# Program order on VectorE and ScalarE between the feed-forward network and the expert loop, with the shared weight parts moved behind the routing

## The chip, the cores and the metric

One core of a Trainium2 chip runs the whole kernel. The metric is the device time of one execution in microseconds (us); the kernel before was run three times. The engines are named as in the profile: PE (TensorE, matrix products), DVE (VectorE), ACT (ScalarE), POOL (GpSimd), and SP (SyncE), which here does nothing but issue the DMAs of the weights. Every engine works off its own instructions in one fixed order; what differs between the two kernels is mostly that order.

## The reference

A two-layer trunk over 256 tokens of width 1024. Layer 0 is attention and a dense SwiGLU network. Layer 1 is a pooling mixer and then eight experts, two of them per token:

```python
for i in range(DEPTH):
    m_lat = (jax.nn.silu(c) @ mod_w[i] + mod_b[i])[:, None, :]
    sh1, sc1, g1, sh2, sc2, g2 = jnp.split(m_lat, 6, axis=-1)
    h_lat = modulate(x, sh1, sc1)                      # h * (1 + scale) + shift
    y_lat = attention_mixer(...) if even else pool_mixer(h_lat, pool_w[j], pool_scale[j])
    x = layer_norm(DEEPNORM_ALPHA * x + g1 * y_lat, ln1_g[i], ln1_b[i])
    h = modulate(x, sh2, sc2)
    y = swiglu(h, ...) if even else moe_swiglu(h, moe_router[j], ...)
    x = layer_norm(DEEPNORM_ALPHA * x + g2 * y, ln2_g[i], ln2_b[i])

def moe_swiglu(h, router, wg, wu, wd):
    top_val, top_idx = lax.top_k(h @ router, TOP_K)    # 2 of 8 experts per token
    ...                                                # softmax of the two, one-hot gates
    for e in range(N_EXPERTS):
        out = out + gates[..., e:e + 1] * swiglu(h, wg[e], wu[e], wd[e])
```

The matrix `mod_w` of a layer has 6 x 1024 columns. The kernel works it off in tiles of 512 columns, the "modulation tiles".

## The kernel before, in words

**Layer 0's feed-forward network** is worked off in chunks of hidden columns, weights streamed from HBM. Each weight tile is split into a rounded part and a remainder (`split`, L154 on ACT, L155 on DVE) and each product is made of three matmuls (`mm3`, L159 to L161). Beside it the twelve modulation tiles of layer 1 are computed, one at a time. A tile can be made on PE (`mod_sums`, L297: 16 matmul records, then one addition on DVE, L331) or on DVE (L336: eight multiply-adds over 512 columns). `next_mod` chooses: tiles 0, 1, 3, 5, 7, 9 and 11 go to PE. The last of them, tile 11, gives the gate row `g2b`; its matmuls stand behind the pooling mixer (L297 and then L356).

**Between the network and the experts**, in this order on PE: the sums over the tokens that the mixer's shift needs (`sums`, L911), the bias rows (L1015), the pooling matmuls (L1024, L1025), the mixer's matmuls (`mix`, L1040), tile 11. DVE adds the residual, takes mean and variance for each half of the tokens and normalizes (`norm` with `rstd1`, L189 to L196 and L1002 to L1009), once before the mixer and once behind it.

**The experts' beginning** (`moe`). The normalized tokens are transposed (L168), modulated and split into a rounded part and a remainder. The router's matmuls (L1150, L1160) give the logits `L`. From them DVE makes, in some twenty small instructions, the selection `sel`, the counts, the ranks and the list `idx`, which says which expert is worked off in which rank. SP reads `idx` (L1260) before it can issue any expert weight's DMA. A first piece of all eight experts, the "head" of 64 hidden columns each, does not depend on the routing: its weights are already on the chip. It is computed in four groups j = 0 to 3, each with a gate part and an up part: `front_parts(j)` splits the weights, `front_sums(j)` does the matmuls (48 for a group), `hidden(j)` multiplies by the gates and applies the activation. Then `gather` picks the tokens of the first step (L1292), and `front(steps[0])` is the first work of the **expert loop** (L1585 gate and up, L1645 back), which streams the rest of the weights, 1 MB a tile, through twelve slots: six of a pool of their own, and six in which the head's weights lie at first.

**What sets the order.** Between `order.enter_context(...)` behind the network's start and `pe_order.close()`, PE's instructions stand as the program is written. DVE's and ACT's are put in order by a scheduler that takes what it expects to be ready first, so that weight splits stand between the small instructions of the routing.

Of the kernel before, what the change touches and what calls it, by code (L numbers as in the profile page):

```python
# [17 lines left out]
P = 128  # L18
D = 1024
KB = D // P  # L20
S = 256
# [81 lines left out]
class Trunk:  # L103
# [79 lines left out]

    def rstd1(self, mv):

        V = self.nc.vector
        one = lambda nm, dt=F32: self.sm.tile([P, 1], dt, name=nm)
        ve, vh, i, y, t, nb = one("ve1"), one("vh1"), one("rsi1", I32), one("rsy1"), one("rst1"), one("nb1")
        V.tensor_scalar(ve, mv[:, 1:2], LN_EPS, None, op0=OP.add)  # L189
        V.tensor_scalar(i, ve.bitcast(I32), 1, None, op0=OP.logical_shift_right)  # L190
        V.tensor_scalar(y.bitcast(I32), i, -1.0, float(0x5f3759df), op0=OP.mult, op1=OP.add)
        V.tensor_scalar(vh, ve, -0.5, None, op0=OP.mult)
        for _ in range(3):
            V.scalar_tensor_tensor(t, y, vh, y, op0=OP.mult, op1=OP.mult)
            V.scalar_tensor_tensor(y, t, 1.5, y, op0=OP.add, op1=OP.mult)
        V.scalar_tensor_tensor(nb, mv[:, 0:1], -1.0, y, op0=OP.mult, op1=OP.mult)  # L196
        return y, nb
# [602 lines left out]
    def residual_stats(self, x, y, alpha=ALPHA):  # L800
# [4 lines left out]
        for h in range(2):  # L805
            for tt in range(2):
# [10 lines left out]
    def layer0_ffn_and_rest(self, xn1):  # L817
        tc, nc, I = self.tc, self.nc, self.I
        with ExitStack() as st0:
# [5 lines left out]
            with ExitStack() as st:  # L825
# [79 lines left out]
                def sums():  # L905

                    m2 = [tmp.tile([P, 4, S], F32, name="wh") for _ in range(2)]
                    for half in range(2):
                        t = self.ps()
                        for s in range(2):  # L910
                            nc.tensor.matmul(t, self.ones, self.A[:, s, 2 * half:2 * half + 2].rearrange("p g t -> p (g t)"), start=(s == 0),  # L911
                                             stop=(s == 1))
                        for c in range(4):
                            k = 4 * half + c
                            nc.scalar.activation(m2[half][:, c], t[:, (c // 2) * S:(c // 2 + 1) * S], AF.Copy, scale=self.ab1[:, 1, k:k + 1])
                    return m2
# [63 lines left out]
                order = ExitStack()  # L980
# [11 lines left out]
                m2 = sums()  # L992

                yp = [[self.acc() for h in range(2)] for tt in range(2)]

                def norm(tt, y, alpha):

                    mv, st = self.sm.tile([P, 2], F32, name="mv1"), self.sm.tile([P, 2, 6], F32, name="bst")
                    for h in range(2):
                        z = x[:, tt, hf(h)]  # L1000
                        if alpha == 1.0:
                            nc.vector.tensor_add(z, z, y(h))  # L1002
                        else:
                            nc.vector.scalar_tensor_tensor(z, z, alpha, y(h), op0=OP.mult, op1=OP.add)
                        nc.vector.bn_stats(st[:, h], z)
                    nc.vector.bn_aggr(mv, st)
                    r, nb = self.rstd1(mv)
                    nc.vector.tensor_scalar(x[:, tt, hf(0)], x[:, tt, hf(0)], mv[:, 0:1], r, op0=OP.subtract, op1=OP.mult)
                    nc.scalar.activation(x[:, tt, hf(1)], x[:, tt, hf(1)], AF.Identity, bias=nb, scale=r)  # L1009

                for tt in range(2):
                    norm(tt, lambda h: accs[tt][h], 1.0)
# [36 lines left out]
            self.moe(x, g2b, head, order)  # L1049
# [32 lines left out]
    def moe(self, xn, g2b, head, pe_order):  # L1082
# [19 lines left out]

        outs = []

        def front_parts(j):
            wg, wu, _ = head[j // 2]
            js = slice((j % 2) * P, (j % 2 + 1) * P)
            parts = []
            for w in (wg, wu):
                wH, wL = [tmp.tile([P, KB, P], F32R, name="wh", bufs=6) for _ in range(2)]  # L1110
                self.split(wH, wL, w[:, :, js])
                parts.append((wH, wL))
            return parts

        with tc.high_priority():
            parts0 = front_parts(0)

        def front_sums(j, between=None):
            parts = front_parts(j) if j else parts0
            outs.append(t := self.ps())  # L1120
            for ks in ([range(2 * k2, 2 * k2 + 2) for k2 in range(4)] if between else [range(KB)]):
                if between:
                    between(ks[0] // 2)
                for (wH, wL), c0 in zip(parts, (0, S)):
                    for k in ks:
                        self.mm3(t[:, c0:c0 + S], wH[:, k], wL[:, k], hd[0][k // 4][:, k % 4], hd[1][k // 4][:, k % 4], k == 0, k == KB - 1)

        zs = []

        def turn(k2):  # L1130
            z = tmp.tile([P, 512], F32, name="a")

            def cp(d, t):
                for u in range(2):
                    self.to_h3(d[:, u * S:(u + 1) * S], t[:, u * S:(u + 1) * S], 2 * k2 + u, V if u else None)
            self.transposes(z, [xn[:, tt, (2 * k2 + u) * P:(2 * k2 + u + 1) * P] for u in range(2) for tt in range(2)], cp)
            self.split(*[h[k2 // 2][:, 2 * (k2 % 2):2 * (k2 % 2) + 2] for h in hd], z.rearrange("p (u q) -> p u q", u=2))
            zs.append(z)


        part = self.acc()
        V.memset(part[:, 0:S], 0.0)

        def route(k2):
            if k2 < 2:
                turn(k2 + 2)
            for u in range(2):
                k = 2 * k2 + u
                q = k % 4
                nc.tensor.matmul(part[q * 32:q * 32 + E, 0:S], self.rt[:, k], zs[k2][:, u * S:(u + 1) * S], start=(k < 4), stop=(k >= 4),  # L1150
                                 skip_group_check=True)

        for k2 in range(2):
            turn(k2)
        front_sums(0, route)
# [516 lines left out]
```

## Time and profile before

| | |
|---|---|
| runs of the kernel before | 1464.86, 1470.41, 1473.06 us (median 1470.41) |
| the profiled execution | 1471.24 us, its span 1469.0 us |
| PE busy in the span | 1370.8 us (93%) |
| DVE busy | 713.9 us (49%) |
| ACT busy | 465.1 us (32%) |
| POOL busy | 105.7 us (7%) |
| read from HBM | 461.87 MB, 315 GB/s over the span |

The profile gives, for one execution, when each instruction ran. A "stretch" below is counted in us from the span's start. PE's share is high, but a share over the span is a mean over stages with different limits: the attention (to about 280), the network (to 485), the stretch of the change (485 to 550) and the expert loop (to 1469). A row of the timeline gives start, length, engine, line, operation, result and operands with their shapes, the count, and in brackets the idle time before it with what ended it.

### The profile page before, as it was taken

To read this page: it belongs to the slowest core of one execution; us is meant where nothing else is said; L and a number is where in the kernel's file an instruction comes from. 1 tells how busy PE (TensorE), PEld (TensorE's weight loads), DVE (VectorE), ACT (ScalarE), POOL (GpSimd) and SP (SyncE) were. 2 spreads that over 40 slices of the span, in tenths; PEclk is the share of its full clock that TensorE was granted. 3 is DMA by queue.
4 is the path that set the end of the run, shared out by engine and by line. 5 is a ranking of instruction groups with operands and counts; after the bars stand their busy time and mean duration, and the time that the engine had idled before them with its cause. 6 is when DMAs were issued, how large, how long until landed. Compare 5 with 4: busy or idle time off the path is not lost. (4 is left out here: it accounts for less than half of the span.)

```text
span 1469.0 us, 22110 instructions
## 1 busy us (share of the span) xinstructions
PE 1370.8 (93%) x8833; PEld 846.9 (58%) x8833; DVE 713.9 (49%) x1158; ACT 465.1 (32%) x692; POOL 105.7 (7%) x65
## 2 busy tenths in 40 slices
PE   6899879699999999999999999999989999999995
PEld 4776546589899685655664333343333345667762
DVE  2678794856767773765573101012110015556663
ACT  3443453443343352544451000010000013445541
POOL 0353050310201000000000000000000000000000
PEclk9999989799999999999999999999999999999998
DMA  9766330698986849999999999999999999999994
GB/s 361 252 194 235 112 105 29 193 374 315 312 301 184 187 146 395 386 393 395 369 370 383 379 394 393 394 345 372 393 393 395 392 362 367 394 389 392 383 350 172
DMA packets 237561, 464.41 MB, mean 316 GB/s; under 512 B 31655, under 2 KB 76922, under 8 KB 237454
## 3 DMA queue, kind: packets, MB, share of 16 engines
q1 hardware_dynamic: 234582, 457.61, 86.7%
q10 hardware_dynamic: 2872, 5.33, 1.2%
q8 instruction: 71, 1.16, 0.3%
q14 instruction: 36, 0.29, 0.1%
HBM read 461.87 MB, written 1.05 MB: 315 GB/s over the span
## 5 line engine op out<-in xcount | busy, mean ns | idle before, releaser
L155 DVE TENSOR_TENSOR wh<-wt,wh 128x1024 fp32r<-128x1024 f32 (+1 forms) x246 | 302.7, 1243 | 94.7 <-ACT wh L154 83.3
L154 ACT CAST wh<-wt 128x1024 fp32r<-128x1024 f32 (+1 forms) x246 | 255.0, 1042 | 219.6 <-PE w L160 84.7
L1585 PE MATMUL w<-wt,xg 128*32 128x256 f32 (+3 forms) x2080 | 231.5, 449 | 14.0 <-DMA wt<-in_moe_w_up_dram 14.0
L1645 PE MATMUL acc<-wt,aT 128*32 128x256 f32 (+2 forms) x1456 | 188.0, 464 | 0.0
L1585 PEld LDWEIGHTS w<-wt,xg 128*32 128x32 f32 (+1 forms) x2080 | 94.2, 120 | 128.4 <-issue 81.7
L1585 PE MATMUL o<-wt,xg 128*64 128x512 f32 (+1 forms) x832 | 133.9, 513 | 2.4 <-DMA wt<-in_moe_w_up_dram 2.4
L1592 DVE TENSOR_TENSOR a<-a,w 64x256 f32<-64x256 f32 (+4 forms) x46 | 23.1, 502 | 223.7 <-ACT a L1591 223.7
L1645 PEld LDWEIGHTS acc<-wt,aT 128*32 128x32 f32 (+2 forms) x1456 | 66.1, 120 | 106.7 <-issue 87.7
L1591 ACT ACTIVATE a<-w 64x256 f32<-64x256 f32 (+4 forms) x46 | 20.2, 439 | 323.6 <-PE w L1585 321.9
L1585 PEld LDWEIGHTS o<-wt,xg 128*64 128x64 f32 (+1 forms) x832 | 46.5, 126 | 75.3 <-issue 64.2
L336 DVE SCALAR_TENSOR_TENSOR raw<-wt,ccol,raw 128x512 f32<-128x512 f32 x91 | 84.6, 930 | 1.6
L160 PE MATMUL w<-hT,wh 128*128 128x256 f32 x272 | 78.3, 288 | 6.2 <-DVE hT L155 6.2
L159 PE MATMUL w<-h2H,wh 128*128 128x256 f32 x272 | 79.2, 291 | 2.4 <-ACT h2H L154 2.4
L161 PE MATMUL acc<-wh,aT 128*128 128x512 f32 x204 | 79.7, 391 | 0.0
L161 PE MATMUL w<-h2H,wh 128*128 128x256 f32 x272 | 77.5, 285 | 0.0
L1592 DVE TENSOR_TENSOR a<-a,o 64x512 f32<-64x512 f32 (+1 forms) x21 | 13.1, 626 | 127.2 <-ACT a L1591 127.2
L160 PE MATMUL w<-wh,xgH 128*128 128x512 f32 (+1 forms) x176 | 70.4, 400 | 3.7 <-DVE wh L155 3.7
L159 PE MATMUL w<-wh,xgH 128*128 128x512 f32 (+1 forms) x176 | 70.3, 400 | 0.0
L1556 POOL TENSOR_TENSOR wt<-wt,ln_g 128x256 f32<-128x256 f32 x1 | 1.0, 1021 | 961.3 <-ACT wt L1554 961.3
L161 PE MATMUL w<-wh,xgL 128*128 128x512 f32 (+1 forms) x176 | 69.2, 393 | 0.0
L1591 ACT ACTIVATE a<-o 64x512 f32<-64x512 f32 (+1 forms) x21 | 11.3, 538 | 164.1 <-PE o L1585 164.1
L160 PEld LDWEIGHTS w<-hT,wh 128*128 128x128 f32 x272 | 53.0, 195 | 7.8 <-DVE hT L155 7.3
(471 smaller groups left out, 2163.9 us busy)
## 6 DMA issues: line engine op xcount, KB each, us to landing
wt<-in_moe_w_down_dram SPq DMA_DIRECT2D x104, 1024.0 KB
wt<-in_moe_w_gate_dram SPq DMA_DIRECT2D x96, 1024.0 KB
wt<-in_moe_w_up_dram SPq DMA_DIRECT2D x96, 1024.0 KB
wt<-in_mod_w_dram SPq DMA_DIRECT2D x45, 1024.0 KB
wt<-in_moe_w_gate_dram SPq DMA_DIRECT2D x16, 896.0 KB
wt<-in_moe_w_up_dram SPq DMA_DIRECT2D x16, 896.0 KB
wt<-in_ffn_w_gate_dram SPq DMA_DIRECT2D x11, 1024.0 KB
wt<-in_ffn_w_up_dram SPq DMA_DIRECT2D x11, 1024.0 KB
```

The lines of the kernel that those rows point to most:

```text
L154: nc.scalar.copy(hi, src)
L155: return (eng or nc.vector).tensor_sub(lo, src, hi.bitcast(F32))
L159: nc.tensor.matmul(out, lh, rh, start=start, stop=False, skip_group_check=True)
L160: nc.tensor.matmul(out, lh, rl, start=False, stop=False, skip_group_check=True)
L161: return nc.tensor.matmul(out, ll, rh, start=False, stop=stop, skip_group_check=True)
L336: nc.vector.scalar_tensor_tensor(acc, w[k], self.ccol[:, k:k + 1], mb if k == 0 else acc, op0=OP.mult, op1=OP.add)
L1556: eng.tensor_mul(o[:, cs], o[:, cs], g[:, hs][:, cs])
L1585: nc.tensor.matmul(t[b:b + M, 0:f1 - f0], xg[:, k], w[k][:, f0:f1], start=(k == 0), stop=(k == KB - 1), skip_group_check=True)
L1591: nc.scalar.activation(a[64:64 + r, f0:f1], t[0:r, f0:f1], AF.Silu)
L1592: nc.vector.tensor_mul(a[0:r, f0:f1], a[64:64 + r, f0:f1], t[64:64 + r, f0:f1])
L1645: nc.tensor.matmul(dacc[0][q2 * M:(q2 + 1) * M, 0:Dn], aT[0:bw, b, q * M:(q + 1) * M], wd[j][0:bw, q2 * Dn:(q2 + 1) * Dn], start=(first an ...
```

## The change

- `next_mod`: tiles 0, 3, 6, 9 and 11 go to PE, the others to DVE.
- `rstd1` is gone. Both residuals go through `residual_stats`, one chain of small instructions for both halves of the tokens, and a `norm` that only normalizes.
- Tile 11's matmuls stand before `mix`, its end behind `mix(0, 0)`. Four matmuls whose result nobody uses stand before the second residual.
- DVE and ACT are in the program's order from the first residual to the end of `leftover`, but for the time in which the head's first two parts are split. PE was so before.
- The head's first part is split by POOL instead of DVE.
- In `moe` all sixteen transposes come first, then the products of part (0, 0), then all router matmuls. Parts (0, 1) and (1, 0) are cut in halves, between which the routing's matmuls stand; the matmuls for the positions are brought forward. Splits of the parts stand at fixed places: (1, 0) before `L`, (1, 1) behind `sel`, (2, 0) and (2, 1) behind the gates, (3, 0) and (3, 1) behind `hidden(1)`. The activation of `hidden(j)` is taken out (`silu(j)`) and stands earlier.

The core of the diff (renamed arguments, the new loops over halves in `sums`, and rows that only move, are left out):

```diff
@@ FFN
-                        self.mod_issue(*mods.pop(0), spool1, n == 0 or n % 2 == 1)
+                        self.mod_issue(*mods.pop(0), spool1, n % 3 == 0 or n == 11)
...
-                m2 = sums()
+                all_order.enter_context(tc.manual_schedule(engines={mybir.EngineType.DVE, mybir.EngineType.Activation}))
+                mv, r, nb = self.residual_stats(x, lambda tt, h: accs[tt][h], 1.0)
+                m2 = [sums(0)]
...
+                assert len(self.mpend) == 1
+                last_mod = self.mpend.pop(0)
+                next(last_mod)
                 for tt in range(2):
                     for h in range(2):
                         mix(h, tt)
-                    norm(tt, lambda h: yp[tt][h], ALPHA)
-                self.mod_finish()
+                        if tt + h == 0:
+                            for _ in last_mod:
+                                pass
+                t = self.ps()
+                for i in range(4):
+                    nc.tensor.matmul(t, self.ones, self.A[:, 0, 0:2].rearrange("p g t -> p (g t)"), start=True, stop=True)
+                mv, r, nb = self.residual_stats(x, lambda tt, h: yp[tt][h])
+                norm(mv, r, nb)
+                all_order.close()
@@ moe
+        def head_part(j, i, eng=None):
+            hl = [tmp.tile([P, KB, P], F32R, name="wh", bufs=6) for _ in range(2)]
+            self.split(*hl, head[j // 2][i][:, :, (j % 2) * P:(j % 2 + 1) * P], eng)
+            return hl
...
+        parts = {(0, 0): head_part(0, 0, nc.gpsimd), (0, 1): head_part(0, 1)}
+        order_of_all.enter_context(tc.manual_schedule(engines={mybir.EngineType.DVE, mybir.EngineType.Activation}))
...
+        head_sums(0, 0, parts[0, 0])
...                                                     # all router matmuls, ps8
+        head_sums(0, 1, parts[0, 1], range(4))
...                                                     # the two matmuls of L
+        head_sums(0, 1, parts[0, 1], range(4, 8))
+        parts[1, 0] = head_part(1, 0)
...                                                     # L, cmp, eq, order, sel
-        front_sums(1)
+        head_sums(1, 0, parts[1, 0], range(4))
...                                                     # counts and positions
+        head_sums(1, 0, parts[1, 0], range(4, 8))
+        parts[1, 1] = head_part(1, 1)
+        head_sums(1, 1, parts[1, 1])
...                                                     # key, rank, perm, eid, idx, pos_r
+        silu(0)
         gate = gates()
-        front_sums(2)
+        for i in range(2):
+            parts[2, i] = head_part(2, i)
+            head_sums(2, i, parts[2, i])
...
         hidden(0)
+        silu(1)
         hidden(1)
-        front_sums(3)
+        silu(2)
+        for i in range(2):
+            parts[3, i] = head_part(3, i)
+            head_sums(3, i, parts[3, i])
         hidden(2)
+        silu(3)
```

DVE from the logits on, before: the splits of the weight parts (L155, `wh`) stand among the small instructions that lead to `sel`.

```order
L1163 COPY L<-acc 128x16
L155 TENSOR_TENSOR wh<-wt,wh 128x1024
L1170 TENSOR_TENSOR cmp<-L 128x128
L1171 TENSOR_TENSOR eq<-L 128x128
L155 TENSOR_TENSOR wh<-wt,wh 128x1024
L1172 TENSOR_TENSOR eq<-eq,cst 128x128
L1435 TENSOR_TENSOR a<-a,w 128x256
L1173 TENSOR_TENSOR cmp<-cmp,eq 128x128
L1175 TENSOR_REDUCE order<-cmp 128x16
L155 TENSOR_TENSOR wh<-wt,wh 128x1024
L1176 TENSOR_SCALAR sel<-order 128x16
```

The same place after the change:

```order
L155 TENSOR_TENSOR wh<-wt,wh 128x1024
L1156 COPY L<-acc 128x16
L1163 TENSOR_TENSOR cmp<-L 128x128
L1164 TENSOR_TENSOR eq<-L 128x128
L1165 TENSOR_TENSOR eq<-eq,cst 128x128
L1166 TENSOR_TENSOR cmp<-cmp,eq 128x128
L1168 TENSOR_REDUCE order<-cmp 128x16
L1169 TENSOR_SCALAR sel<-order 128x16
L155 TENSOR_TENSOR wh<-wt,wh 128x1024
```

Three splits and a product have left this piece; one split stands before `L`, one behind `sel`. From `key` to `idx`, where one split and two more products stood, there are now only the seven small instructions.

ACT behind the routing, after the change (L1252 is the activation of `silu`, L1218 the exponential of the gates; `wh` are weight splits, `xg` those of the hidden values): the casts of part (2, 0) and (2, 1) stand behind the exponential, those of (3, 0) and (3, 1) behind `silu(2)`.

```order
L154 CAST wh<-wt 128x1024 x2
L1252 ACTIVATE a<-o 128x256
L1218 ACT_TABLE_LOAD
L1218 ACTIVATE ex<-ex 128x2
L154 CAST wh<-wt 128x1024 x2
L191 DMA ln_g<-in_ln_g_dram 128x1024
L191 DMA ln_b<-in_ln_b_dram 128x1024
L154 CAST xg<-a 128x256
L1252 ACT_TABLE_LOAD
L1252 ACTIVATE a<-w 128x256
L154 CAST xg<-a 128x256
L1252 ACTIVATE a<-w 128x256
```

Before, the scheduler set the casts of `wh` between these, each as soon as its buffer was free.

PE around the mixer, after the change (L282 is tile 11, L341 its end, L1031 the four matmuls nobody uses, L1113 the transposes):

```order
L282 MATMUL w<-wt,cS 32x512 x8
L1016 MATMUL acc<-pw,hT 128x256 x4
L341 MATMUL w<-raw,four 128x512
L1016 MATMUL acc<-pw,hT 128x256 x12
L1031 MATMUL w<-A,ones 128x512 x4
L1113 MATMUL o<-cst,xn_85 128x128 x4
L1113 MATMUL w<-cst,xn_85 128x128 x12
```

And before:

```order
L1040 MATMUL acc<-pw,hT 128x256 x16
L297 MATMUL w<-wt,cS 32x512 x8
L356 MATMUL o<-raw,four 128x512
L168 MATMUL w<-cst,xn_85 128x128 x8
L168 MATMUL o<-cst,xn_85 128x128 x4
```

Tile 11 has moved from behind the mixer into it.

## Rows read from the trace of the kernel before

**Rows 1.** Windows: stretch, length, busy us of each engine, clock, DMA share, GB/s

```profile
283.00:485.00 202.00, 202.00 (x1451) 180.21 (x1450) 130.47 (x169) 77.43 (x106) 19.25 (x13) 1.00 0.84 280
500.00:540.00 40.00, 35.34 (x242) 28.59 (x241) 31.32 (x102) 17.51 (x25) 0.00 (x0) 0.91 0.25 73
```

**Rows 2.** What PE waits for in the expert loop, from 540 on

```profile
PE w L1585 <- DMA wt<-in_moe_w_up_dram: 14.0, 4, 3.8
```

**Rows 3.** What SP's queue waits for, 440 to 700: us, times, longest

```profile
SPq L1260 <- DVE idx L1195: 39.7, 1, 39.7
...
SPq L128 <- PE acc L1645: 23.6, 6, 9.4
```

**Rows 4.** Groups by line in the feed-forward network, DVE: splits and modulation tiles

```profile
L155 DVE TENSOR_TENSOR wh<-wt,wh 128x1024 fp32r<-128x1024 f32 x59 | 74.9, 1272 | 44.2 <-ACT wh L154 40.5 <-PE w L297 1.6 <-PE o L297 1.6
...
L336 DVE SCALAR_TENSOR_TENSOR raw<-wt,ccol,raw 128x512 f32<-128x512 f32 x35 | 26.2, 749 | 0.6
```

**Rows 5.** Timeline of PE around the mixer

```profile
497.59 7.07 PE L1040 MATMUL acc<-pw,hT 128*128 128x256 f32 x32
...
504.59 1.92 PE L297 MATMUL w<-wt,cS 128*32 128x512 f32 x16
...
507.78 1.12 PE L356 MATMUL o<-raw,four 128*128 128x512 f32 x2 [1.26 <-DVE raw L331]
...
511.35 0.87 PE L168 MATMUL w<-cst,xn 128*128 128x128 f32 x6 [2.33 <-DVE xn L1008]
```

**Rows 6.** Timeline of DVE, the two-column chain in layer 0, first and last

```profile
258.36 0.33 DVE L814 BATCH_NORM_AGGREGATE bmv<-bst 128x2 f32<-128x12 f32 x2
...
261.17 0.81 DVE L200 TENSOR_SCALAR xn<-xn,bmv,rsy 128x1024 f32<-128x1024 f32 x1
```

**Rows 7.** Window behind the first transposes

```profile
512.40:519.20 6.80, 5.73 (x24) 3.84 (x22) 4.69 (x8) 3.70 (x7) 0.00 (x0) 0.50 0.48 174
```

**Rows 8.** Timeline of DVE in the routing

```profile
526.20 0.17 DVE L1163 COPY L<-acc 128x16 f32<-128x16 f32 x1 [1.50 <-PE acc L1160]
526.31 1.22 DVE L155 TENSOR_TENSOR wh<-wt,wh 128x1024 fp32r<-128x1024 f32 x1
...
531.24 0.17 DVE L1176 TENSOR_SCALAR sel<-order 128x16 f32<-128x16 f32 x1
...
535.61 0.17 DVE L1195 CAST idx<-eid 128x8 int32<-128x8 f32 x1
...
536.74 0.17 DVE L1211 TENSOR_SCALAR pos_r<-pos_r 128x16 f32<-128x16 f32 x1
```

**Rows 9.** Timeline of SP's queue in the loop's beginning

```profile
536.79 0.98 SPq L128 DMA_DIRECT2D wt<-in_moe_w_gate_dram  x2
...
588.08 3.43 SPq L128 DMA_DIRECT2D wt<-in_moe_w_down_dram  x2
...
601.43 1.00 SPq L128 DMA_DIRECT2D wt<-in_moe_w_gate_dram  x2
```

**Rows 10.** Window from the first expert load to the wait at 601

```profile
536.80:601.40 64.60, 61.15 (x338) 42.49 (x339) 37.00 (x81) 27.52 (x43) 0.00 (x0) 0.97 1.02 382
```

**Rows 11.** Timeline of PE from the head to the first step

```profile
538.56 1.22 PE L1432 MATMUL acc<-cst,sl 128*128 128x128 f32 x8
...
545.27 0.60 PE L1432 MATMUL acc<-cst,sl 128*128 128x128 f32 x4
...
549.82 7.09 PE L1585 MATMUL w<-wt,xg 128*64 128x512 f32 x32
```

**Rows 12.** Timeline of ACT behind the routing

```profile
540.90 1.28 ACT L1434 ACT_TABLE_LOAD   x1 [0.20 <-DVE xg L155]
...
542.52 1.05 ACT L154 CAST wh<-wt 128x1024 fp32r<-128x1024 f32 x1
```

**Rows 13.** Timeline of DVE and POOL before the network, a split beside POOL

```profile
268.95 3.37 DVE L155 TENSOR_TENSOR wh<-wt,wh 128x1024 fp32r<-128x1024 f32 x1
...
265.70 5.53 POOL L867 TENSOR_TENSOR xn<-xn,row 128x1024 f32<-128x1024 f32 x2 [8.27 <-PE o L168]
```

More of the change, by code (lines that the diff above doesn't have):

```diff
@@ L182, in rstd @@
         return r, nb
[L184 to L197, printed above, removed]
     def normalize(self, x, mv, r, nb):
@@ L804, in residual_stats @@
         st = [self.sm.tile([P, 2, 6], F32, name="bst") for tt in range(2)]
-        for h in range(2):
-            for tt in range(2):
+        for tt in range(2):
+            for h in range(2):
                 z = x[:, tt, h * 512:(h + 1) * 512]
@@ L903, in between, with sums @@
                             G.tensor_add(ab[:, 1], ab[:, 1], mc[:, sh])
[L905 to L915, printed above, removed]
+                def sums(half):
+                    t, m2 = self.ps(), tmp.tile([P, 4, S], F32, name="wh")
+                    for s in range(2):
+                        nc.tensor.matmul(t, self.ones, self.A[:, s, 2 * half:2 * half + 2].rearrange("p g t -> p (g t)"), start=(s == 0),
+                                         stop=(s == 1))
+                    for c in range(4):
+                        k = 4 * half + c
+                        nc.scalar.activation(m2[:, c], t[:, (c // 2) * S:(c // 2 + 1) * S], AF.Copy, scale=self.ab1[:, 1, k:k + 1])
                     return m2
@@ L978, in chunk @@
                     between(c)
[L980 removed]
+                order, all_order = ExitStack(), ExitStack()
                 order.enter_context(tc.manual_schedule(engines={PE}))
@@ L1115, in moe @@
[L1115 to L1138, printed above, removed]
+        def head_sums(j, i, w, ks=range(KB)):
+            if i == 0 and ks[0] == 0:
+                outs.append(self.ps())
+            o = outs[j][:, i * S:(i + 1) * S]
+            for k in ks:
+                self.mm3(o, w[0][:, k], w[1][:, k], hd[0][k // 4][:, k % 4], hd[1][k // 4][:, k % 4], k == 0, k == KB - 1)
@@ new lines, in moe @@
+        parts = {(0, 0): head_part(0, 0, nc.gpsimd), (0, 1): head_part(0, 1)}
+        order_of_all.enter_context(tc.manual_schedule(engines={mybir.EngineType.DVE, mybir.EngineType.Activation}))
+        zs = [tmp.tile([P, 512], F32, name=nm) for nm in ("a", "a", "aT", "aT")]
+        zp = [self.ps() for _ in range(4)]
+        for k2 in range(4):
+            for j, (u, tt) in enumerate((u, tt) for u in range(2) for tt in range(2)):
+                nc.tensor.transpose(zp[k2][:, j * P:(j + 1) * P], xn[:, tt, (2 * k2 + u) * P:(2 * k2 + u + 1) * P], self.ident)
@@ L1141, in moe @@
+        modulated(1, 1, V)
+        lo(0)
+        modulated(1, 0)
+        hi(1)
+        modulated(2, 1, V)
+        lo(1)
+        modulated(2, 0)
+        hi(2)
+        modulated(3, 1, V)
+        lo(2)
+        modulated(3, 0)
+        hi(3)
+        lo(3)
+        head_sums(0, 0, parts[0, 0])
         part = self.acc()
         V.memset(part[:, 0:S], 0.0)
[L1144 to L1151, printed above, removed]
@@ L1153, in moe @@
-        for k2 in range(2):
-            turn(k2)
-        front_sums(0, route)
+        for k in range(KB):
+            q = k % 4
+            nc.tensor.matmul(part[q * 32:q * 32 + E, 0:S], self.rt[:, k], zs[k // 2][:, (k % 2) * S:(k % 2 + 1) * S], start=(k < 4), stop=(k >= 4),
+                             skip_group_check=True)
         ps8 = gat.tile([P, NT, 224], F32, name="sl")[:, :, 0:P]
         V.tensor_copy(ps8, part[:, 0:S].rearrange("p (t q) -> p t q", t=2))
+        head_sums(0, 1, parts[0, 1], range(4))
```

63 lines of the change are left out of this document (29 added, 34 removed).

## The prediction

> **What bounds the kernel now.** The page's shares say little, since the stages have different limits, so I read the windows first. In the feed-forward network PE is busy 202.0 of 202.0 us and DMA only to 0.84 [rows 1]: there each us taken from PE is a us won. From 500 to 540 PE is busy 35.3 of 40 us and DMA to 0.25 [rows 1]: neither is at its limit, the routing's chain is. The waits of SP's queue name it: 39.7 us for `idx`, the longest wait around the change [rows 3]. No expert weight moves before. From then on both are full: of the loop's 929 us PE stands 14.0 for the main group of weight tiles [rows 2], and SP in turn waits for PE to give back slots [rows 3]. So two things leave the change's stretch and count for the end: when the loads start (before: `idx` at 535.61 [rows 8], first issue 536.79 [rows 9]) and when PE starts the first step (549.82 [rows 11]).
>
> How much slack there is between the two, I read from SP's queue. From 536.79 to 588.08 stand twelve rows of two tiles each, then the queue waits until 601.43 [rows 9] for the first step's last matmuls, 9.4 us [rows 3]. Those 24 tiles of 1.049 MB are 25.2 MB; in the same 64.6 us 382 GB/s moved 24.7 MB [rows 10]. Only 0.5 MB, 1.3 us of work, was left in the queue. A PE that is over 1.3 us later there makes the loads later.
>
> **FFN.** Of tiles 1, 5, 7 and 6, three leave PE and one comes: two fewer, 1.92 us each [rows 5], 3.8 us. DVE gets 2 x 8 multiply-adds of 0.749 us [rows 4], 12.0 us, beside its 130.5 of 202 [rows 1]; it stands 44.2 us before the splits waiting for ACT [rows 4], which covers that. If the cover is gone, because two of DVE's tiles now follow each other, PE waits for splits and nothing is won. I take -3.6, between -3.8 and 0. The pooling's end, 497.6 [rows 5], becomes 494.0.
>
> **Mixer and second norm.** Tile 11 (1.92) and its end (1.12) come in front of or into the mixer's 7.07 us [rows 5], so it ends 10.1 us behind the pooling and not 7.1. Before, they lay beside DVE's norm; that cover is given up. From the mixer's end to the transposes were 6.7 us (504.66 to 511.35 [rows 5]). Now: the last addition and statistics, two passes over 512 columns at about 0.75 as the multiply-adds [rows 4], 1.5; one chain for both halves, 258.36 to 261.17, 2.8; normalizing two halves at 0.81, 1.6 [rows 6]. That is 5.9, and 16.0 behind the pooling against 13.8: +2.2. From below -0.8, if tile 11 hides whole; from above +4.4, if the split on POOL meets the one that DVE has left there: beside a POOL multiplication a DVE split took 3.37 us [rows 13] and not 1.22 [rows 8]. I take +2.2, since DVE has to wait for the mixer at that place anyway. The first transpose is at 510.0 and not 511.35.
>
> The Trainium skill, "SBUF — State Buffer", section "SBUF: two separate sides", states that VectorE and GpSimd hold a shared port pair exclusively for an instruction, also where VectorE reads two SBUF operands. The trace agrees with its 3.37 us; by the page the upper end would hold, and the sum would be 2.2 us more.
>
> **Routing.** Before: 14.85 us from the transposes to `L`, 9.4 from `L` to `idx` (526.20, 535.61 [rows 8]). Among the latter stood four splits of 1.22, two products and pieces of the gates; one split stays, behind `sel`, where DVE has to wait for the counts anyway. 9.4 less three splits (3.7) and less about 0.9 for the rest is 4.8. Before `L`, a quarter of a group's matmuls goes, about 1.4 of 5.5 us (a group is what stands between 539.78 and 545.27 [rows 11]). That makes 18.3. In 512.4 to 519.2 the granted clock was 0.50 [rows 7], the level of 1.2 GHz, just behind PE's waits of 1.26 and 2.33 [rows 5]; at full clock up to 3.4 us less. I take 17, between 15 and 19: `idx` at 527.0, 8.6 us earlier, first issue 528.2.
>
> **Behind `idx`.** Here the program's order costs. Before, PE went without a wait from the routing to the first step, since the scheduler put each split where a buffer was free. Now:
> - Parts (2, 0) and (2, 1) are split on DVE behind 26 rows of positions and gates. A dependent chain runs at 2.8 us for 14 steps, 0.2 each [rows 6]: 5.2, with a product and the exponential's way over ACT 6.0, and the split 1.2. The sums start at 527.0 + 7.2 = 534.2, where PE has been idle some 4 to 5 us.
> - The sums, 5.5, until 539.7.
> - Then `hidden(0)`, `silu(1)`, `hidden(1)`, `silu(2)` and the split of (3, 0) are one chain over three engines: a table load 1.28 and a cast 1.05 [rows 12], a split 1.22, twice 0.6 on PE [rows 11], and some eight steps over 256 columns of 0.4 (half of the 0.749 for 512 [rows 4]): 8.0, in which PE works 1.2. Until 547.7.
> - The sums of (3, *), 5.5, until 553.2.
> - `hidden(2)`, gather and `hidden(3)`: before 4.55 (545.27 to 549.82 [rows 11]); now `silu(3)` and a product stand ahead of the gather's masks in DVE's order, some 2 more: 6.5.
> The first step starts at 559.7, 9.9 us later than before. If half of the waits vanished it would be 5 later, if the clock fell in them up to 7 more (below).
>
> **To the end.** The loads lead by 8.6 us, but only ten tiles of them have slots without the first step: twelve slots less the two whose head weights go last. Ten tiles at 382 GB/s take 27.5 us: until 555.7. The next slot is free in the first step's middle, 559.7 + 3.5 = 563.2. Before, the tenth tile was through at 536.8 + 27.5 = 564.3. So DMA runs dry for 7 to 8 us and its lead is gone before the loop has begun. At 601 then PE is 9.9 late against a slack of 1.3: the loads go on 8.6 late, and from there both sides are full, and the 14.0 us of waits for weights are no reserve, because the weights are late too. Sum: +8.6 on the profiled execution's 1471.24 (span 1469.0 and 2.2 around it), which lies 0.8 above the median of 1470.41: 1479 us.
>
> **Rivals.**
> - *The early start carries* (faster). If the first step starts before about 552, a slot is free before the ten tiles are through, DMA never runs dry, and the end comes with the loads: 1470.4 - 8.6 = 1462. For it: 39.7 us is the largest wait [rows 3], and the loop is full of DMA. Against: it needs the waits behind `idx` to be some 8 us shorter than my sum.
> - *Break-even.* PE regains the lag in the first steps, where it was not full, and the dry stretch just eats the lead: about 1471. For it: 61.15 of 64.6 us are busy [rows 10], so 3.4 us can be regained, and the chain of 8.0 may overlap more than I count. Against: these waits are for DVE in the first step, not for weights.
> - *The clock falls in the new gaps* (slower still). PE idles 4 to 5 us, and then 7 us in two pieces, longer than the waits ahead of the half clock in [rows 7]. Each fall costs 6.8 us at half speed, 3.4 us, in the sums, where PE is the path: 1482 to 1486. The same time comes out if the network's 3.6 is not won, 1483.
> The Trainium skill, "TensorE: Matmul & The Clock Gate", Part 1, says that the array goes to 1.2 GHz when it has been idle and back when it is busy again. The trace shows just that at 512.4; by the page the last rival would be the forecast.
> - *The change does not do what it says.* The order of the instructions stands in the program; only the time of `idx` can miss.
>
> **How the numbers follow.** Forecast 0.45 with its own range 1474 to 1483; early start 0.15; break-even 0.22; clock or network 0.18. About 0.5%, 7.4 us, is what a measurement of this kernel can tell from no change: under 1463.1 or over 1477.8. Faster: the early start without its upper edge, 0.13. Slower: two thirds of the forecast, 0.30, the last rival 0.18, and the upper edge of break-even 0.02, 0.50. The rest, 0.37, is within. For 8 in 10 the range reaches from 1463 to 1487; it leaves out the best of the early starts and both clock falls with all other bounds.
>
> **What would show it.** Right: PE still full from 283 to the network's end, which comes 3 to 4 us earlier; `idx` at 525 to 529; PE's waits for DVE's `wh` or ACT of over 10 us between `idx` and the first step; the first step at 557 to 562; a stretch around 556 to 563 in which DMA moves nearly nothing. The forecast is wrong if the first step starts before 553, if DMA does not run dry before it, or if the wait at 601 does not move; and the network's part is wrong if PE waits there for `wh`.

## The result and the profile after

Six runs of the changed kernel: median 1480.91 us (1476.37 to 1484.11); six of the kernel before beside them: 1468.18 (1464.86 to 1473.06). The ratio is 1.008, 95% interval 1.0051 to 1.011: slower by 7.5 to 16 us. The forecast was 1479, slower, by 8.6. The ratios and medians here and below leave out two executions in a slower state of the chip, 1746.59 us of the kernel before and 4212.48 us of e3.

The profiled execution after took 1480.74 us, its span 1478.7. One thing first, or all starts are misread: layer 0's first transposes stand at 262.03 before and at 258.37 after, at the same wait of 5.51 us. The change does nothing ahead of them but swap two loops in `residual_stats`, and the chain that leads to them is the same in both traces. Everything behind them is therefore 3.7 us earlier for a reason that is not the change: run again, the changed kernel has them at 260.76, and the kernel before with one later line changed (e5) at 257.42. Starts are compared below as distances from this point ("from the mark"). In the timeline of PE before it is this row (start, length, line, operation, shapes; in brackets the idle time before):

```profile
262.03 2.94 PE L168 MATMUL w<-cst,xn 128*128 128x128 f32 x12 [5.51 <-DVE xn L200]
```

Timeline of PE, after:

```profile
258.37 2.94 PE L168 MATMUL w<-cst,xn 128*128 128x128 f32 x12 [5.51 <-DVE xn L185]
...
477.83 1.88 PE L894 MATMUL w<-A,ones 128*128 128x512 f32 x4
...
490.24 1.92 PE L282 MATMUL w<-wt,cS 128*32 128x512 f32 x16
...
505.66 0.91 PE L1113 MATMUL o<-cst,xn 128*128 128x128 f32 x4 [2.10 <-DVE xn L982]
...
535.02 0.61 PE L1438 MATMUL acc<-cst,sl 128*128 128x128 f32 x4
538.96 0.82 PE L1438 MATMUL acc<-cst,sl 128*128 128x128 f32 x4 [3.33 <-DVE sl L1437]
541.94 0.58 PE L159 MATMUL w<-xgH,wh 128*128 128x256 f32 x1 [2.17 <-ACT wh L154]
...
552.57 1.58 PE L1298 MATMUL o<-sl,xn 128*128 128x64 f32 x8 [1.91 <-DVE sl L1292]
...
560.17 8.61 PE L1595 MATMUL o<-wt,xg 128*64 128x512 f32 x32
570.62 0.50 PE L159 MATMUL acc<-wh,xg 128*128 128x512 f32 x1 [1.85 <-ACT wh L154]
...
586.89 3.65 PE L1655 MATMUL acc<-wt,aT 128*64 128x512 f32 x16
```

The same two places, the network's end and the first step's back, in the trace before:

```profile
485.42 3.60 PE L911 MATMUL w<-A,ones 128*128 128x512 f32 x8
...
572.10 3.65 PE L1645 MATMUL acc<-wt,aT 128*64 128x512 f32 x16
```

The network ends (L894) 219.5 from the mark, before (L911) 223.4: 3.9 less. The transposes stand 15.4 behind the pooling's end (490.24), before 13.8 [rows 5]. The first step (L1595) starts at 301.8 from the mark, before at 287.8 [rows 11]: 14.0 later. Its back (L1655) stands at 328.5, before (L1645) at 310.1: 18.5 later.

Timeline of DVE after, the instructions of [rows 8] and the splits behind them:

```profile
516.41 0.17 DVE L1156 COPY L<-acc 128x16 f32<-128x16 f32 x1 [0.37 <-PE acc L1151]
...
518.12 0.17 DVE L1169 TENSOR_SCALAR sel<-order 128x16 f32<-128x16 f32 x1
...
521.17 0.17 DVE L1195 CAST idx<-eid 128x8 int32<-128x8 f32 x1
...
526.70 2.35 DVE L155 TENSOR_TENSOR wh<-wt,wh 128x1024 fp32r<-128x1024 f32 x2
...
535.67 0.42 DVE L1440 TENSOR_TENSOR a<-a,acc 128x256 f32<-128x256 f32 x1 [6.34 <-PE acc L1438]
...
541.92 2.36 DVE L155 TENSOR_TENSOR wh<-wt,wh 128x1024 fp32r<-128x1024 f32 x2 [0.46 <-ACT wh L154]
```

`L` to `idx` takes 4.8 us, not 9.4; `idx` is at 262.8 from the mark, before 273.6: 10.8 earlier. Then the price: the two splits of part 2 stand 5.5 us behind `idx`, then DVE stands 6.34 us until PE's sums are through, and PE in turn waits for DVE and ACT. What PE waits for from the network's end to the first step's first product:

```profile
PE acc L1438 <- DVE sl L1437: 3.3, 1, 3.3
PE w L159 <- ACT wh L154: 3.1, 2, 2.2
PE w L161 <- DVE wh L155: 2.3, 2, 1.9
...
PE o L1298 <- DVE sl L1292: 1.9, 1, 1.9
PE acc L159 <- ACT wh L154: 1.8, 1, 1.8
```

Between `idx` and the first step these are 10.6 us (the first four rows; the fifth stands behind the first step's start). Before, the trace shows none there.

ACT in the same place has long idle times, each a link of the chain over three engines:

```profile
536.12 0.41 ACT L154 CAST xg<-a 128x256 fp32r<-128x256 f32 x1 [9.62 <-DVE a L1440]
536.54 1.28 ACT L1252 ACT_TABLE_LOAD   x1
...
540.85 1.98 ACT L154 CAST wh<-wt 128x1024 fp32r<-128x1024 f32 x2
```

Windows after: the network, the stretch that answers to the second of [rows 1], and three in which PE runs wholly or in part at half its clock (columns as there; third last the granted clock):

```profile
283.00:477.80 194.80, 194.80 (x1391) 176.44 (x1391) 142.91 (x182) 75.71 (x103) 17.69 (x13) 1.00 0.88 291
500.00:540.00 40.00, 30.07 (x207) 24.98 (x205) 25.59 (x84) 13.32 (x19) 0.00 (x0) 0.95 0.43 156
530.00:535.00 5.00, 5.00 (x34) 5.00 (x34) 0.00 (x0) 0.00 (x0) 0.00 (x0) 0.75 1.02 370
539.40:546.20 6.80, 4.17 (x19) 3.58 (x18) 3.81 (x7) 2.57 (x4) 0.00 (x0) 0.50 1.03 398
553.00:563.70 10.70, 10.70 (x45) 8.09 (x45) 2.18 (x10) 3.20 (x9) 0.00 (x0) 0.52 0.07 27
```

PE was full to the network's end, as before. From 500 to 540 it is busy 30.1 of 40 us, before 35.3 [rows 1]. From 539.4 to 546.2 and from 553 on the granted clock is 0.50, the level of 1.2 GHz, the first time behind the wait of 3.33 us, the second behind that of 1.91. A shorter stretch stands ahead of them: in the products of group 2, from 529.1 to 532.4, the clock is 0.51, behind waits of 0.93 and 1.87 us, and 16 matmuls start 0.21 us apart and not 0.12, which costs 1.5 us. And in the last of the stretches DMA moves next to nothing. SP's queue, which answers to [rows 9], its wait for the first step's products, and the transfers from 520 to 640, in forty equal slices of 3 us:

```profile
522.38 0.99 SPq L128 DMA_DIRECT2D wt<-in_moe_w_gate_dram  x2
...
531.36 3.76 SPq L128 DMA_DIRECT2D wt<-in_moe_w_gate_dram  x2
543.17 1.51 SPq L128 DMA_DIRECT2D wt<-in_moe_w_up_dram  x2
565.37 0.99 SPq L128 DMA_DIRECT2D wt<-in_moe_w_down_dram  x2
...
612.34 1.01 SPq L128 DMA_DIRECT2D wt<-in_moe_w_gate_dram  x2
...
SPq L128 <- PE o L1595: 22.4, 2, 20.5
...
GB/s 5 227 408 380 373 400 409 399 388 386 386 96 0 0 0 106 411 410 387 386 391 218 149 193 157 302 396 388 393 408 218 231 402 386 389 382 398 399 386 388
```

The first load goes out at 522.38, but behind ten tiles (the last pair at 543.17) the queue stands until 565.37, 20.5 us of it for the first step, and DMA is dry from about 555 to 565.

### The profile page after: what moved, and what is told of

It is laid out like the page before. It is cut to its first block, busy times and chain, and to the rows that moved or that the text cites. A ratio compares the mean times of both kernels' runs of the same rounds, so it can differ in the third digit from the quotient of the medians.

```text
span 1478.7 us, 22061 instructions
## 1 busy us (share of the span) xinstructions
PE 1370.7 (93%) x8809; PEld 850.5 (58%) x8809; DVE 728.4 (49%) x1154; ACT 464.8 (31%) x691; POOL 106.3 (7%) x66
## 5 line engine op out<-in xcount | busy, mean ns | idle before, releaser
L155 DVE TENSOR_TENSOR wh<-wt,wh 128x1024 fp32r<-128x1024 f32 (+2 forms) x245 | 299.9, 1238 | 81.7 <-ACT wh L154 74.9
L1595 PE MATMUL w<-wt,xg 128*32 128x256 f32 (+3 forms) x2496 | 314.6, 468 | 16.3 <-DMA wt<-in_moe_w_up_dram 16.3
L1595 PEld LDWEIGHTS w<-wt,xg 128*32 128x32 f32 (+1 forms) x2496 | 121.1, 122 | 177.7 <-issue 123.5
L1655 PE MATMUL acc<-wt,aT 128*32 128x256 f32 (+2 forms) x1456 | 188.2, 464 | 0.0
L1602 DVE TENSOR_TENSOR a<-a,w 64x512 f32<-64x512 f32 (+4 forms) x58 | 31.2, 538 | 308.3 <-ACT a L1601 308.3
L1601 ACT ACTIVATE a<-w 64x512 f32<-64x512 f32 (+4 forms) x58 | 27.1, 467 | 430.9 <-PE w L1595 429.2
L1655 PEld LDWEIGHTS acc<-wt,aT 128*32 128x32 f32 (+2 forms) x1456 | 67.1, 120 | 105.6 <-issue 85.7
L321 DVE SCALAR_TENSOR_TENSOR raw<-wt,ccol,raw 128x512 f32<-128x512 f32 x105 | 102.2, 975 | 2.1
L160 PE MATMUL w<-wh,xgH 128*128 128x512 f32 (+1 forms) x144 | 57.2, 397 | 1.4 <-DVE wh L155 1.4
L159 PEld LDWEIGHTS w<-h2H,wh 128*128 128x128 f32 x288 | 55.7, 193 | 3.4 <-ACT h2H L154 2.6
L159 PE MATMUL w<-wh,xgH 128*128 128x512 f32 (+1 forms) x144 | 57.3, 398 | 0.0
L161 PEld LDWEIGHTS w<-h2H,wh 128*128 128x128 f32 x288 | 55.9, 194 | 0.0
L1595 PE MATMUL o<-wt,xg 128*32 128x256 f32 (+2 forms) x416 | 50.7, 467 | 0.0
L159 PE MATMUL acc<-wh,aH 128*128 128x512 f32 (+1 forms) x112 | 45.3, 404 | 0.0
```

The source lines that it names most:

```text
L155: return (eng or nc.vector).tensor_sub(lo, src, hi.bitcast(F32))
L159: nc.tensor.matmul(out, lh, rh, start=start, stop=False, skip_group_check=True)
L160: nc.tensor.matmul(out, lh, rl, start=False, stop=False, skip_group_check=True)
L161: return nc.tensor.matmul(out, ll, rh, start=False, stop=stop, skip_group_check=True)
L321: nc.vector.scalar_tensor_tensor(acc, w[k], self.ccol[:, k:k + 1], mb if k == 0 else acc, op0=OP.mult, op1=OP.add)
L1595: nc.tensor.matmul(t[b:b + M, 0:f1 - f0], xg[:, k], w[k][:, f0:f1], start=(k == 0), stop=(k == KB - 1), skip_group_check=True)
```

## The experiments

Starts are from the mark, in us; "pair 13" is the load behind the first 24 tiles, at which the queue waited before (601.43 [rows 9]). The ratio is to the kernel before, from runs on the same chip.

| kernel | `idx` | first step | its back | pair 13 | ratio (95%) |
|---|---|---|---|---|---|
| before | 273.6 | 287.8 | 310.1 | 339.4 | 1 |
| after | 262.8 | 301.8 | 328.5 | 354.0 | 1.008 (1.0051 to 1.011) |
| after, again | 263.1 | 300.9 | 328.5 | 353.9 | 1.0112 (1.0097 to 1.0127) |
| scheduler behind `pos_r` (e1) | 266.2 | 283.3 | 305.6 | 331.0 | 0.9941 (0.9918 to 0.9965) |
| after, late `idx` (e2) | 270.7 | 301.8 | 328.7 | 354.2 | 1.0104 (1.0079 to 1.0129) |
| after, fillers (e3) | 262.9 | 297.5 | 324.3 | 349.7 | 1.0083 (1.0059 to 1.0108) |
| the same, again | 263.1 | 296.1 | 322.7 | 348.1 | 1.008 (1.0062 to 1.0097) |
| other program order (e4) | 263.0 | 291.7 | 318.5 | 344.0 | 1.0037 (1.0019 to 1.0055) |
| before, network's line alone (e5) | 270.0 | 284.2 | 306.5 | 335.8 | 0.9984 (0.9965 to 1.0002) |
| after, scheduler from the first step (e6) | 262.8 | 302.9 | 326.2 | 351.7 | 1.0072 (1.0048 to 1.0097) |
| e1 with `idx` ahead of splits (e7) | 263.4 | 283.6 | 305.9 | 331.3 | 0.9947 (0.9929 to 0.9965) |
| e1, late `idx` (e8) | 275.1 | 284.0 | 312.4 | 338.7 | 0.9984 (0.9969 to 0.9999) |
| e4, fillers, scheduler from the first step (e9) | 262.8 | 291.6 | 313.9 | 339.3 | 1.0007 (0.9993 to 1.0021) |

In every row the time by the ratio moved as pair 13 did, to within some 3 us: what counts for the end is when the queue gets past this place.

**e1. Program order only up to the positions.**

```diff
-        order_of_all.close()          # behind leftover
+        order_of_all.close()          # behind pos_r, ahead of silu(0)
```

> The changed kernel, but VectorE and ScalarE go back to the scheduler's order right behind the positions of the tokens (pos_r), not behind the whole head. Theory (the program's order behind idx makes the first step late, and the late first step eats the early start of the loads): idx stays early, within 2 us of the changed kernel's 521; the first step starts at 542 to 548, not 560; DMA does not run dry in front of it; 18 to 22 us less than the changed kernel, ratio to the kernel before 0.990 to 0.996. Rival (the loss comes from ahead of idx, or from the network): the first step may come earlier, but the ratio stays at 1.005 to 1.010.

Measured: the first step 18.5 us earlier than after, the ratio 0.9941, 1456.66 us against 1466.4: faster than both kernels. The waits of the list above are gone; PE's waits from the transposes to the first step:

```profile
PE o L160 <- DVE ymoe L1121: 0.7, 2, 0.3
PE o L159 <- issue: 0.5, 1, 0.5
```

and DMA, in the slices of 520 to 640, does not stop:

```profile
GB/s 5 0 214 401 388 388 407 403 386 386 386 405 406 386 383 386 397 410 394 387 386 388 406 391 391 387 388 402 407 388 388 386 398 403 394 388 386 393 403 403
```

So what the change does to the network and up to the positions is, taken together, a gain; the loss comes from the program's order behind them. `idx` itself came 3.4 us later than after (266.2), more than the 2 us expected, since the scheduler put two splits ahead of it.

**e2 and e8. The same late `idx` in two kernels.** In e2 the conversion to `idx` stands behind the splits of part (2, 1); in e8, on e1, it is fed by a product of `hidden(1)` times zero.

```diff
 # e2, on after
-        V.tensor_copy(idx, eid)       # behind eid
+        V.tensor_copy(idx, eid_k)     # behind head_part(2, 1)
 # e8, on e1
+        V.scalar_tensor_tensor(eid_l, silus[1][:, 0:8], 0.0, eid_k, op0=OP.mult, op1=OP.add)
+        V.tensor_copy(idx, eid_l)     # behind hidden(1)
```

> The changed kernel, but the conversion that makes idx stands behind the splits of part (2, 1) in VectorE's order, so that SP reads it some 8 us later; all else stays. Theory (the lead of the loads is eaten by the first step's lateness): the first expert load is issued some 8 us later, the dry stretch ahead of the first step (555 to 565 in the changed kernel) shrinks by as much, and the time stays within 2 us of the changed kernel, ratio 1.006 to 1.010. Rival (the loads' start sets the end): 8 us more, ratio 1.013 to 1.014.

> The first experiment's kernel (scheduler behind pos_r), but idx is made to depend on the product of hidden(1), so that SP reads it 6 to 10 us later; the computed value is the same. Counterpart of the changed kernel's late idx. Theory (the loads' start sets the end once the first step is early): 5 to 9 us more than the first experiment, ratio 0.998 to 1.001. Rival (the loads' start never counts, the first step does): no more than 2 us, ratio 0.993 to 0.996.

Measured: e2, 7.9 us later with `idx`, has 1.0104 against 1.008 and 1.0112 of the changed kernel: no loss that can be told, and pair 13 goes out at the same place (354.2 against 354.0). e8, 9.0 us later with `idx`, has 0.9984 against 0.9941, 6.3 us more, with a first step that starts only 0.7 later; in it PE then waits 3.4 us for a weight tile, and its back is 6.8 later. The first loads of e2 and e8:

```profile
527.67 0.99 SPq L128 DMA_DIRECT2D wt<-in_moe_w_gate_dram  x2
...
540.56 4.51 SPq L128 DMA_DIRECT2D wt<-in_moe_w_up_dram  x2
562.92 0.99 SPq L128 DMA_DIRECT2D wt<-in_moe_w_down_dram  x2
```
```profile
529.86 0.99 SPq L128 DMA_DIRECT2D wt<-in_moe_w_gate_dram  x2
...
541.26 6.00 SPq L128 DMA_DIRECT2D wt<-in_moe_w_up_dram  x2
547.50 5.66 SPq L128 DMA_DIRECT2D wt<-in_moe_w_down_dram  x2
```

In e2 the queue stops all the same behind ten tiles until 562.92, the first step's doing; in e8 it goes on. The dry stretch of e2 shrank by some 5 us and not by the 8 expected: its last pair ahead of the stop goes out at 284.8 from the mark, just as in the changed kernel, so part of the lead was gone before. The loads' start counts where the first step is early, and not where it is late.

**e3. The clock alone.** Matmuls of no use in PE's waits behind `hidden(0)`, `hidden(1)` and `hidden(2)`:

```diff
         hidden(0)
+        fill(8)      # 8 times matmul(t[:, 0:S], self.ones, iota)
         silu(1)
         hidden(1)
+        fill(6)
         silu(2)
...
         hidden(2)
+        fill(6)
         silu(3)
```

> The changed kernel with 8, 6 and 6 matmuls of 256 columns whose result nobody uses, on PE behind the matmuls of hidden(0), hidden(1) and hidden(2), where PE stands. Theory: the waits themselves stay, but the half clock at 539 to 546 and at 553 to 564 goes away, which costs some 7 us now; the first step starts 4 to 8 us earlier (552 to 556) and the end comes 4 to 8 us earlier, ratio 1.003 to 1.006. Rival one (the clock has no part in it): first step and ratio stay, 560 and 1.008. Rival two (the first step's time has no part in the end): the first step is earlier, the ratio stays at 1.008.

The windows that answer to the two of half clock above:

```profile
540.00:546.80 6.80, 6.21 (x41) 5.49 (x40) 4.21 (x10) 2.57 (x4) 0.00 (x0) 1.00 1.03 400
553.00:563.70 10.70, 10.70 (x69) 6.20 (x67) 2.18 (x10) 3.21 (x9) 0.00 (x0) 1.00 0.37 124
```

The clock stays at 1.00 where it was 0.50, and the first step is 4.3 us earlier. (Ahead of the fillers, from 530.6 to 534.0, it is 0.53 here too.) The ratio, 1.0083, did not show it: a miss. Both kernels were therefore run once more beside each other:

> The changed kernel again, beside its own version with filler matmuls on one chip, because the two ratios so far (1.008 and 1.0083) were taken against different runs of the kernel before. Expected by all theories: 1.006 to 1.010, the first step 301 to 303 us behind layer 0's first transposes.

> The changed kernel with the filler matmuls, again, beside the changed kernel on one chip. Theory (the half clock is on the path): 3 to 6 us less than the changed kernel beside it, as the first step is 4.3 us earlier in the trace. Rival (the first step's time does not come through to the end): within 1.5 us of it.

Here 1476.22 against 1482.62 us, 1.008 against 1.0112: 4.7 us by the ratios, as the traces have it (the first step is 4.8 earlier). The intervals just touch, but each of the six times with fillers (1480.69 at most) lies under each of the four without (1480.82 at least). The changed kernel's own ratio, 1.0112, lies a little over the 1.006 to 1.010 expected. So beside each other the two kernels show the gain, which the first ratio, without the changed kernel beside it, did not; that the half clock delays the first step by some 4 us is shown by the traces.

**e4. Another program order, written by hand.**

```diff
         V.tensor_copy(idx, eid)
+        parts[2, 0] = head_part(2, 0); head_sums(2, 0, parts[2, 0])
...                                    # pos, by_rank(pos_r)
-        silu(0)
+        parts[2, 1] = head_part(2, 1); head_sums(2, 1, parts[2, 1])
         gate = gates()
+        silu(0); silu(1)
+        parts[3, 0], parts[3, 1] = head_part(3, 0), head_part(3, 1)
+        head_sums(3, 0, parts[3, 0])
         hidden(0); hidden(1); silu(2)
+        head_sums(3, 1, parts[3, 1])
         hidden(2); ...                # gather, then silu(3) and hidden(3)
```

> The changed kernel, still in the program's order, but the program is written otherwise behind idx: split and products of part (2, 0) right behind idx, of (2, 1) behind pos_r, then the gates, both activations (0) and (1), both splits of group 3, hidden(0) and hidden(1) between the products of (3, 0) and (3, 1). Theory (not program order as such but these chains keep PE waiting): PE waits under 4 us in all between idx and the first step, which starts at 541 to 547; DMA does not run dry; ratio 0.990 to 0.996. Rival (only a scheduler fills these gaps): the first step stays behind 552, ratio over 1.002.

A miss: PE waits less, 5.3 us between `idx` and the first step and not 10.6, but not under 4, and the first step is 10 us earlier than after, but at 291.7 and not at e1's 283.3. The ratio, 1.0037, is the rival's. What is left shows in PE's timeline:

```profile
531.90 0.68 PE L1443 MATMUL acc<-cst,sl 128*128 128x128 f32 x4 [1.64 <-DVE sl L1442]
...
537.43 1.11 PE L1303 MATMUL o<-sl,xn 128*128 128x64 f32 x8 [1.57 <-DVE sl L1297]
538.37 4.73 PE L1303 MATMUL w<-sl,xn 128*128 128x64 f32 x24
544.84 1.19 PE L1443 MATMUL acc<-cst,sl 128*128 128x128 f32 x4 [1.75 <-DVE sl L1442]
...
556.51 0.50 PE L159 MATMUL acc<-wh,xg 128*128 128x512 f32 x1 [1.85 <-ACT wh L154]
```

Three waits of 1.6 to 1.8 us, and again the half clock, 0.50 from 540 to 545: the gather's 24 matmuls take 4.73 us, which took 2.79 before. The fourth wait stands behind the first step's start, where the program's order is still in force.

**e5. The network's line alone, on the kernel before.**

```diff
-                        self.mod_issue(*mods.pop(0), spool1, n == 0 or n % 2 == 1)
+                        self.mod_issue(*mods.pop(0), spool1, n % 3 == 0 or n == 11)
```

> The kernel before with one line of the change alone: modulation tiles 0, 3, 6, 9 and 11 on PE. Theory (PE sets the network's time and two tiles leave it): from the first transposes of layer 0 behind the attention to the network's end 3.5 to 4.0 us less than in the kernel before (223.4), all that follows 3.5 to 4.0 us earlier, ratio 0.9965 to 0.9985. Rival (VectorE's two tiles in a row make PE wait for splits, or what is won is eaten behind): under 1.5 us, ratio 0.999 to 1.001.

From the mark to the network's end 218.9, 4.5 less, a little over the 3.5 to 4.0 expected; `idx` and the first step 3.6 earlier; ratio 0.9984, 2.3 us less, in the range expected, but with 1 just inside the interval. PE stays full:

```profile
283.00:482.00 199.00, 199.00 (x1397) 177.49 (x1396) 147.94 (x209) 79.19 (x112) 18.20 (x13) 1.00 0.89 291
```

**e6. The scheduler's order from the first step on.**

```diff
+        order_of_all.close()          # it stood behind leftover
         accs = [[self.acc() for h in range(2)] for tt in range(2)]
         a = front(steps[0])
```

> The changed kernel, but VectorE and ScalarE are back in the scheduler's order just ahead of the first step's front, not behind leftover. Theory (program order costs behind the first step's start too: PE waits 1.85 and 0.76 us there, since ScalarE's casts for the head's last product stand behind the first step's activation): from the start of the first step to its back 22 to 24 us, not 26.7; the first step starts within 1 us of the changed kernel's; 2 to 5 us less in all, ratio 1.004 to 1.007. Rival (only the order ahead of the first step counts): 26 to 27 us there, ratio 1.008 to 1.010.

From the first step's start to its back 23.3 us, not 26.7, and before 22.3; the waits of 1.85 and 0.76 us at 570.62 and 571.88 are gone. The ratio, 1.0072, is within noise of 1.008: the 2 to 5 us expected are not shown by the time.

**e7. `idx` ahead of the two splits, on e1.**

```diff
         V.tensor_copy(idx, eid)
+        parts[2, 0] = head_part(2, 0); head_sums(2, 0, parts[2, 0])
...                                    # pos, by_rank(pos_r)
+        parts[2, 1] = head_part(2, 1); head_sums(2, 1, parts[2, 1])
         order_of_all.close()
```

> Scheduler's order behind the head's middle as in the first experiment, but split and products of part (2, 0) stand in program order right behind idx, those of (2, 1) behind pos_r, and the program's order ends there; so the two splits that the scheduler put ahead of idx stand behind it. Theory (with an early first step the loads' start sets the end): idx 2 to 3 us earlier than there, the first step within 1.5 us, ratio 0.990 to 0.994, that is 1 to 3 us under the first experiment. Rival (PE has become the bound again): ratio as there, 0.994 to 0.996.

`idx` is 2.7 us earlier, the first step where it was, the ratio 0.9947: the rival's. The lead of the loads is used up here too: the ninth pair goes out at 565.23 (307.9 from the mark) and in e1 at 565.70 (307.6), and pair 13 at 331.3 against 331.0.

**e9. e4 with fillers in its waits, and without the order behind the first step.** Added to e4:

```diff
         hidden(0)
+        fill(6)
...
         hidden(2)
+        fill(6)
...                                    # gather
+        fill(6)
         silu(3)
         hidden(3)
+        order_of_all.close()          # it stood behind leftover
```

> The hand-written order of the fourth experiment with the two other terms taken away as well: six matmuls of 256 columns whose result nobody uses in each of PE's three waits behind idx, and the scheduler's order again from the first step's front on. Theory (three terms make up the whole loss behind idx: the chains that PE waits for, the half clock behind them, and the order behind the first step's start): granted clock 1.00 from idx to the first step; from layer 0's first transposes to the first step 285 to 288 us (there 291.7), to its back 307 to 311 (there 318.5); DMA dry for under 2 us; ratio 0.993 to 0.999. Rival (something else of the program's order costs): back behind 313, ratio over 1.001.

A miss in part. The clock is 1.00, PE has no wait over 0.5 us between `idx` and the first step, and from there to its back it takes 22.3 us as before; but the first step is no earlier (291.6, expected 285 to 288): the fillers take 8.3 us, more than the 5.3 us of waits that they fill, and nobody uses what they compute. The back at 313.9 is the rival's, the ratio of 1.0007 lies between the two. That three terms make up the whole loss is therefore not shown, and whether a hand-written order without fillers can reach e1 is left open.

## Why the prediction was right, and where its sizes were off

**The mechanism held.** `idx` early, first step late, DMA dry between, and the end set by the late first step: each is in the trace after, and e1, e2 and e8 tell it from the rivals. Two signs were missed in size: `idx` came at 521.17, 262.8 from the mark, which would be 524.8 in the trace before and lies ahead of the 525 to 529 named; and of PE's 10.6 us of waits only 5.4 are for `wh`, the rest for the small copies that feed the gates and the gather (`sl`). The early start does not carry where the first step is late (e2); it does where it is early (e8). The rival that had it carry is what e1 became: `idx` 7.4 us earlier from the mark than before, and 8.7 us less time.

**The slack rule** of 1.3 us at the first long wait for the loop's back, 601.43 before [rows 9]: that wait ends at 612.34 after, 354.0 from the mark and not 339.4, 14.6 later. Less 1.3 that is 13.3, and the end of the span stands 13.4 later from the mark (1478.7 - 258.37 against 1469.0 - 262.03). That it fits so closely is luck: in the changed kernel's second execution the wait ends at 353.9 too, and the span's end stands 17.3 later (1485.0 - 260.76). Two executions differ by more than the rule's 1.3, so it is not tested by this.

**The network**, -3.6: measured -3.9, and -4.5 in e5. DVE's idle time did cover the two tiles. **The mixer**, +2.2: 15.4 against 13.8, +1.7. **The split on POOL**, the upper end of that term: it did not meet a split of DVE. It lay beside a residual addition of DVE, which took its usual time (0.67 to 0.69 us in all eight):

```profile
496.71 0.69 DVE L796 SCALAR_TENSOR_TENSOR xn<-xn,acc 128x512 f32<-128x512 f32 x1 [1.17 <-PE acc L1016]
```
```profile
496.65 2.36 POOL L155 TENSOR_TENSOR wh<-wt,wh 128x1024 fp32r<-128x1024 f32 x1 [4.91 <-ACT wh L154]
```

**The routing**, 17: measured 15.5 (505.66 to 521.17), at the lower end; the half clock that stood behind the transposes before (0.50 in [rows 7]) is not there, the granted clock is 1.00 from 500 to 525. Whether the four unused matmuls behind the mixer keep it there was not tried.

**Behind `idx`** the sum was 32.7 us to the first step, and 39.0 were measured. The chains are right: the sums of group 2 end 13.9 behind `idx` (12.7 in the sum; 1.5 of it is half clock), the chain to group 3 takes 6.9 (8.0). What was mis-sized stands behind them: group 3's sums took 8.1 us, not 5.5, and the rest to the first step 10.1, not 6.5, both in part at 0.50. That the first step's 560.17 lies so near the 559.7 of the forecast is luck, the 3.7 us by which this trace is early at the mark. I had the clock as a rival of 0.18 with 3.4 us for each fall, and it is part of what happened; in the trace the two later stretches cost about 4 us (e3: 4.3 earlier without them). The Trainium skill, "TensorE: Matmul & The Clock Gate", Part 1, has the array at 1.2 GHz after it has been idle; the stretches of 0.50 behind waits of 3.33 and 1.91 us agree, the 1.00 behind the wait of 2.10 us does not show it. The lesson is that a forecast which makes PE idle should carry this price in its sum, not beside it.

**A step was missing.** From the first step's start to its back I took the time of before, and it was 4.4 us longer: 1.5 for the first products, at half clock until 563.7 (8.61 us against 7.09 [rows 11]), and 2.6 for two waits (1.85 and 0.76), because ACT's casts for the head's last product stand behind the first step's activation as long as the program's order holds (e6: gone with it). I had looked at what the order does up to the first step, and it was in force beyond.

Both together made PE 18.5 us late at the first step's back, where the forecast had 9.9. PE regained 3.9 of it up to the wait at 601 (14.6 there), and so the traces' ends are 13.4 apart and the runs 11.7 (0.8% of 1468), not 8.6. The size was off by a quarter to a third, on the side of too little; that 1479 lies so near to 1480.91 owes something to the median of before, which moved from 1470.41 to 1468.18 with more runs.

## What to carry to other kernels

Program order on all engines here shortened a chain of small dependent instructions (`L` to `idx` 9.4 to 4.8 us) and lengthened the stretch in which several independent chains could overlap (`idx` to the first step 14.2 to 39.0; 28.7 with the better order of e4). Hold it only over the chain, and give the rest back to the scheduler, which here made a loss of 0.8% a gain of 0.6%. Before you pull a transfer's start forward, count the buffers: here the lead was worth only the ten tiles that had a slot without the consumer. And follow a fixed order to where it ends in the program, not to where its purpose ends.

## What the runs showed of the hardware that was not expected

The clock did not follow the length of a wait alone. In the changed kernel it stayed at 1.00 behind a wait of 2.10 us (505.66), and was 0.50 behind those of 3.33 and 1.91; in e4 it was 0.50 from 540 to 545 behind waits of 1.64 and 1.57. Nor was it the same in two executions of one kernel: behind the waits of 0.93 and 1.87 us in group 2's products it fell to 0.51 in the changed kernel and to 0.53 in e3, and in the second execution of each, behind the same two waits, it was 1.00. With fillers in the later waits it was 1.00 from there to the first step (e3, both executions), and in e9 from `idx` on.
